# Prompt attention of a hybrid decoder step: queries split behind a shared transpose, and all eight key tiles of a group kept on chip

## The chip, the core and the metric

The kernel runs on one core of a Trainium2 chip, as one launch. The metric is device time in microseconds (us) of that core; the median of three runs stands for the kernel. A core has five engines with instruction queues of their own: TensorE (PE, with its weight loads shown as PEld), VectorE (DVE), ScalarE (ACT), GpSimd (POOL) and SyncE (SP), which here issues the DMA transfers. Each engine works through its queue in order and waits on semaphores.

## What is computed

One inference step of a two-layer decoder, for a prompt of 1024 rows and for 8 sample rows. Layer A is a gated delta rule with a convolution; layer B is sliding-window attention, and the change lies in layer B's part for the prompt. Cut to that:

```
def swa_layer(x, kb, vb, dist, valid, norm_g, w_in, q_norm, sinks, w_out):
    q, gate = jnp.split(rmsnorm(x, norm_g) @ w_in, 2, axis=-1)
    q = rmsnorm(q.reshape(b, L, N_Q_HEADS, HEAD_DIM), q_norm)          # 16 heads of 64
    q = q.reshape(b, n_blk, L // n_blk, N_KV_HEADS, Q_GROUP, HEAD_DIM) # 4 groups of 4 heads
    o = windowed_sink_attention(q, kb, vb, dist, valid, sinks).reshape(b, L, ATT_W)
    o = o * jax.nn.silu(gate)
    return x + o @ w_out

def windowed_sink_attention(q, k, v, dist, valid, sinks):
    s = einsum('bnqhgd,bnshd->bnhgqs', q, k) * HEAD_DIM ** -0.5
    s = where(valid, s - slopes * dist, -inf)          # a query block of 128 sees its own and the previous key block
    mx = maximum(max(s), sink); p = exp(s - mx)
    p = p / (sum(p) + exp(sink - mx))
    return einsum('bnhgqs,bnshd->bnqhgd', p, v)
```

Keys and values are projected once, from the residual stream behind layer A, for 4 key/value heads of 64; each is shared by a group of 4 query heads. All is float32.

## The kernel before, in words

**Precision.** A float32 product is made of passes over parts that the type float32r holds exactly: a value is copied to float32r (the high part, on ACT), the rest is subtracted (the low part, on DVE), and high times high, high times low and low times high are summed in PSUM. `split` (line 82) and `load_split` (line 87) do this for weights: the piece of 512 columns is loaded by SP, scaled by a gain on POOL (line 100), copied on ACT (line 83) and subtracted on DVE (line 84).

**The attention stage.** Behind layer A the program runs `load_qkv`, `sample_qkv`, `tile_qkv`, `gate_load` and `gate_group` over 4 groups of heads. Per group 256 columns of query weights, 64 of key and 64 of value weights are loaded and split (tile `wqkv`, two buffers), and the 1024 rows are taken in 8 tiles of 128. `tile_qkv` (line 1172) is a generator of three stages that the loop at line 1288 interleaves (`PIPE`): the stages of up to three tiles and the gate's projections (`gate_group`, 24 matmuls into the bank `ivY`) are issued alternately. The stages of tile t are:

1. 24 matmuls of 384 columns into `ps` (line 1178); the heads' mean squares (`head_stats`); the normed queries `qn`, 128 rows by 4 heads by 64 (DVE, line 1184); `qhl`, which puts each head's high part and low part side by side (high: ACT, line 1187; low: DVE, line 1188); the normed keys `kn`, twice side by side (DVE, line 1191). Then 4 transposes on PE, one per head, turn the 128 rows by (64 high + 64 low) into (64 high + 64 low) partitions by 128 rows, in PSUM (`tq`, line 1199), and ACT copies the 512 columns to `qst` (line 1201). The keys are transposed once (line 1203) and split into `kTh` (ACT, 1205) and `kTl` (DVE, 1206).
2. Scores: for each head two matmuls, `qst` against `kTh` and against `kTl` (lines 1225 and 1226). As `qst` holds high and low on two halves of the partitions and the keys stand on both halves, one matmul gives (high + low) times a part of the key. Then bias and maximum (DVE, 1229), exponentials and their scaling (ACT, 1239 and 1245).
3. Transposes of the probabilities in float32 (`ptp`, line 1252), copies (`pt`), and the product with the values (`op`, line 1262), which DVE multiplies into the gate (`oT`, line 1264).

**Keys on chip.** `kTh` and `kTl` hold `RK` = 4 tiles of 128 keys as a ring. A tile needs its own and the previous tile's keys. Where the two stand side by side the matmul has 256 columns; at t = 4 the ring wraps, the two are apart, and each head has four matmuls of 128 columns (`kcuts`, line 1208). At t = 0 there is no previous tile, and each head has two matmuls of 128.

**The output projection.** Tiles `oh` (line 1314) hold the attention's result of a row tile in parts; the weights `wob` come in three chunks of 384, 384 and 256 columns (line 1405). For each chunk and row tile: the residual is loaded (`hx5`, line 1419, two buffers; shown as `hx<-hD`), 24 matmuls run, DVE adds (line 1430) and SP stores (line 1435). The first tiles of the first chunk use the gate's one PSUM bank, the others two banks `pj`. PE starts on this while the last attention tiles are still in work.

**What sets the order.** In this stage the order of the instructions in each engine's queue is worked out when the program is built: a planner with costs of its own follows the program's order and lets an instruction ahead when the ones before it are still waiting. Buffers of closed pools are given to later pools, and a later tile waits for the last use of each earlier tile whose bytes it takes. On the left side of SBUF stand, in this order, the projected rows' inputs `ng` (24,576, 24,576 and 16,896 bytes a partition) with `hs` (1,280), then the attention's pool `at_`; behind them the output stage's 8 tiles `oh` take 65,536 bytes from the same start and the pool `p5` follows. `bp` (with `oT`, 32,768 bytes), the raw weights and the gate's weights `gw` (two buffers of 8,192) stand on the right side.

Of the kernel before, what the change touches and what calls it, by code (L numbers as in the profile page):

```python
# [20 lines left out]
P = 128  # L21
# [10 lines left out]
HD = 64  # L32
EPS = 1e-6
NEG = -1.0e30
RK = 4  # key tiles kept on chip
K1 = 6  # heads whose output is projected before the last two are done
# buffers
NB = 4  # half heads between their preparation and the chain
TFB = 2  # inverses ahead of the chain
QB = 3  # heads of convolved queries  # L40
NY = 3  # tiles of the last projection's first chunk that use the gate's bank
RB = [2, 2, 4]  # pieces of raw weights in flight: delta rule, output projection A, attention
LG = 2  # heads whose gate is projected last
# order of loads and of tiles
LO = "0g12k345q678"  # x's tiles, the norm's gain, the first key's and query's weights
CT = 5  # the x tile after which the convolution's taps are transposed
P3O = [0, 1, 2, 3, 8, 4, 5, 6, 7]
# stages of an attention tile and the tiles that each lags behind; the gate's tiles ahead
PIPE = [(1, 1), (0, 0), (2, 2)]
GA = 1  # L50
# what a stage's results are taken to need on the other engines (ns), and the priorities there
HOP = [1000, 900, 1200, 1000, 900, 1000, 900, 900]
# [6 lines left out]
def hybrid_step(  # L59
# [25 lines left out]

    # float32 products are three passes over parts that float32r holds exactly: hi * hi + hi * lo + lo * hi
    def load_split(hi, lo, src, gain=None):
        # src [P, k, c] in pieces of at most 512 a partition, scaled by gain [P, k] if there is one
        _, nk, c = src.shape
        n = min(512 // c, nk)  # L90
        for k in range(0, nk, n):
            pool = raws[-1]
            if len(raws) == 2:
                # both pools are open while the output projection's weights come in
                pool = raws[alt[0] % (RB[0] + RB[1]) >= RB[0]]
                alt[0] += 1
            raw = pool.tile([P, 512], F32, tag="raw", name="raw")[:, :n * c].rearrange("p (k c) -> p k c", c=c)
            DMA.dma_start(out=raw, in_=src[:, k:k + n])
            if gain is not None:
                G.tensor_tensor(out=raw, in0=raw, in1=gain[:, k:k + n].unsqueeze(2).broadcast_to([P, n, c]), op=ALU.mult)  # L100
            split(hi[:, k:k + n], lo[:, k:k + n], raw)
# [24 lines left out]

    # ---------------------------------------------------------------- constants
    ident = cst.tile([P, P], F32, name="ident")
# [4 lines left out]
    V.memset(ones, 1.0)  # L133
    # 1/sqrt(scale*src + eps): the first guess from the exponent's bits, a step of Newton's and one of third order
    NR0, NR1 = 2.38924456, 0.703952253
# [21 lines left out]

    # ---------------------------------------------------------------- phase 1: x -> normalised, transposed
    es2 = ExitStack()
# [9 lines left out]
    whl = es2w.enter_context(tc.tile_pool(name="whl", reuse_waits="tile", bufs=2, side="right"))  # L169
    # ---------------------------------------------------------------- phase 2a: decays, betas, taps  # L170
    p2 = es2.enter_context(tc.tile_pool(name="p2", reuse_waits="tile", bufs=1))
# [3 lines left out]
    mgtr = p2.tile([P, P], F32R, name="mgtr")  # L175
    # +1 on the diagonal, -1 right of it in the even rows: the inverse of the 2x2 blocks, transposed
    par = p2.tile([P, 1], F32, name="par")
# [231 lines left out]

    # ---------------------------------------------------------------- phase 2: projections, conv, delta rule  # L410
    gd = es2.enter_context(tc.tile_pool(name="gd", reuse_waits="tile", bufs=2))

    # The tensor engine's work from here to the output projection is cut into streams: generators that issue one stage
    # at a time and yield the time (ns) that the stage's results take on the other engines. run() merges them into the
    # tensor engine's order: a stage comes once its operands are due, and the projections fill the time between.
    due = {"decay": D0}
# [229 lines left out]
    def inverse(h):  # L646
# [3 lines left out]
        def clear(li):  # L650
            # zeroes what a level leaves unwritten in its blocks; the two tiles alternate
            b = lvls[li]
            z_ = xlv[li % 2].bitcast(F32)
            if b <= 16:
                z_ = z_.rearrange("p c (n s w) -> p c n s w", s=2, w=b // 2)[:, :, :, 1, :]
            G.memset(z_, 0.0)  # L656
# [154 lines left out]
    def norm_stream():  # L811
        for n_ in range(2 * H):
            h, hf = divmod(n_, 2)
            yield from need(("c", n_))
            d = dd[n_]
            osb, oss = d["osb"], d["oss"]
            # the query's norm enters only as the weight of the output norm's guard
            with tc.high_priority(offset=PN):
                x_ = sm.tile([P, 4], F32, tag="f1", name="f1")
                V.scalar_tensor_tensor(out=x_, in0=oss, scalar=NRS / 128.0, in1=d["xq"], op0=ALU.mult, op1=ALU.add)  # L820
                f2 = sm.tile([P, 4], F32, tag="f2", name="f2")
                u_ = sm.tile([P, 4], F32, tag="fu", name="fu")
                rsqrt_x(f2, x_, u_)
                V.tensor_tensor(out=osb, in0=osb, in1=f2.unsqueeze(2).broadcast_to(B4), op=ALU.mult)
            yield YN
            yield from need(("z", h))
            otp = gps("otp")
            for c in range(4):
                tr(otp[:, ts(c, P)], osb[:, c, :], ident)
            ov = hd[h]["og"][:, ts(hf, 512)]  # L830
            V.scalar_tensor_tensor(out=ov, in0=otp, scalar=ogain, in1=ov, op0=ALU.mult, op1=ALU.mult)
            yield (("n", n_), 700)
# [103 lines left out]

    # ---------------------------------------------------------------- phase 3: output projection A, residual, norm
    def zero_r(t_, scr):
# [126 lines left out]

    # ---------------------------------------------------------------- phase 4: shared K/V, q, gate, windowed attention
    bp = ctx.enter_context(tc.tile_pool(name="bp", reuse_waits="tile", bufs=1, side="right"))
# [29 lines left out]
    V.tensor_scalar_mul(distm, distm, -1.0)  # L1097
    identr = at_.tile([P, P], F32R, name="identr", bufs=1)
    V.tensor_copy(identr, ident)
    islp = at_.tile([P, NQH], F32, name="islp", bufs=1)  # L1100
# [16 lines left out]
    def gate_group(m, w_, gi):  # L1117
        # twice the gate's SiLU: g * (1 + tanh(g / 2)); the half goes into the product with the attention's output
        g0, gn = GRP[gi]
# [52 lines left out]
    def tile_qkv(g, t, w_):  # L1172
# [3 lines left out]
        for a, b in ((0, 0), (0, 1), (1, 0)):  # L1176
            for k in range(KT):
# [7 lines left out]
                        in1=r5[:, 0:4].unsqueeze(2).broadcast_to(s4), op=ALU.mult)  # L1185
        qhl = at_.tile([P, 4, 2, HD], F32R, tag="qhl", name="qhl", bufs=1)
        S.copy(qhl[:, :, 0, :], qn)
        V.tensor_tensor(out=qhl[:, :, 1, :], in0=qn, in1=qhl[:, :, 0, :].bitcast(F32), op=ALU.subtract)
        kn = at_.tile([P, 2, HD], F32, tag="kn", name="kn")
# [4 lines left out]
        if t == NT - 1:  # L1194
            DMA.dma_start(out=k_win_p[0, :, g, :], in_=kn[:, 0, :])
            DMA.dma_start(out=v_win_p[0, :, g, :], in_=vsb[:, t % 4, :])
        tq = chp.tile([P, 512], F32R, tag="chA", name="tq")
        for h in range(4):
            PE.transpose(tq[:, ts(h, P)], qhl[:, h].rearrange("p a d -> p (a d)"), identr)  # L1199
        qst = at_.tile([P, 512], F32R, tag="qst", name="qst")  # L1200
        S.copy(qst, tq)
        tk = ps[:, 384:512]
# [15 lines left out]
        for hp_ in range(2):  # L1218
            sps = gps("sps")
            s_ = at_.tile([P, 2, 2 * P], F32, tag="s_", name="s_", bufs=3)  # L1220
            for i in range(2):
                h = 2 * hp_ + i
                for k0, o_, nk in kcuts:
                    ov = sps[:, i * 256 + o_:i * 256 + o_ + nk]
                    mm(ov, qst[:, ts(h, P)], kTh[:, k0:k0 + nk], True, False)
                    mm(ov, qst[:, ts(h, P)], kTl[:, k0:k0 + nk], False, True)
            for i in range(2):
# [79 lines left out]

    # ---------------------------------------------------------------- sample attention and output projection B
    es5 = ExitStack()
# [95 lines left out]
    for ci, (c0, cn) in enumerate(CHK):  # L1405
# [10 lines left out]
        for t in list(range(NT)) + [NT]:  # L1416
            samp = t == NT
            n = NS if samp else P
            hx = bp.tile([P, 384], F32, tag="hx5", name="hx5", bufs=2)
            DMA.dma_start(out=hx[:n, :cn], in_=hD[t * P:t * P + n, c0:c0 + cn])  # L1420
# [48 lines left out]
```

## Time and profile before

| What | Value |
| --- | --- |
| Runs of the kernel (us) | 1325.66, 1326.26, 1332.1 |
| Median (us) | 1326.26 |
| Span of the profiled execution, first to last instruction (us) | 1323.5 |
| Mean granted TensorE clock in it, share of 2.4 GHz | 0.983 |
| Busy share of the span: PE, PEld, DVE, ACT, POOL | 93%, 85%, 72%, 48%, 23% |

The profiled execution is known by its span; the median of the runs is 2.8 us above it. Busy shares are means over stages with different limits. Matmuls are pipelined, and the duration that is shown for one runs to its modelled end, so what a matmul costs PE is read from the distance between starts. Where the profile says "idle before", the engine stood still, and the name behind the arrow is what ended the wait.

### The profile page before, as it was taken

The page shows a single profiled execution, that of the slowest core. Times are in us where ns is not written, and L with a number is a line of the kernel's source. Part 1 is how long each engine was busy: PE and PEld are TensorE (multiplying, and loading weights), DVE is VectorE, ACT ScalarE, POOL GpSimd, SP SyncE. Part 2 cuts the span into 40 slices and gives each one's busy share as a digit, 9 for nine tenths or more (in the row PEclk, how much of TensorE's full clock was granted, in tenths as well). Part 3 has the DMA queues.
Part 4 walks back from the last instruction along what each step waited for, and adds up shares of the span by engine and source line. Part 5 has one row for each costly group of instructions (what it writes and reads, how often), then busy time and mean ns, then how long its engine had stood idle before and what let it go on. Part 6 is the DMA issues. An engine that isn't in the chain of part 4 may idle for free.

```text
span 1323.5 us, 24515 instructions
## 1 busy us (share of the span) xinstructions
PE 1236.9 (93%) x8923; PEld 1122.8 (85%) x8923; DVE 949.1 (72%) x2897; ACT 635.6 (48%) x1822; POOL 299.1 (23%) x400
## 2 busy tenths in 40 slices
PE   4997989899999999998999999899999999999998
PEld 3987878898888899898887886798888888888898
DVE  7567878887888789888977548667686686777221
ACT  5343444635536455464654227365575575677100
POOL 1115442332334324344411002202011010000000
PEclk9998999999999999999999999999998999999999
DMA  7021201102021031110144437302011021102322
GB/s 249 19 65 32 58 25 50 51 17 84 17 84 33 17 85 30 56 49 17 51 143 144 149 134 244 87 26 56 4 50 32 3 57 31 45 1 72 128 90 72
DMA packets 124068, 87.89 MB, mean 66 GB/s; under 512 B 34152, under 2 KB 115792, under 8 KB 123888
## 3 DMA queue, kind: packets, MB, share of 16 engines
q1 hardware_dynamic: 123948, 86.33, 22.1%
q8 instruction: 70, 1.15, 0.4%
q14 instruction: 50, 0.41, 0.1%
HBM read 65.11 MB, written 23.28 MB: 67 GB/s over the span
## 4 chain that ended last, share of the span: by engine, by line
PE 63%; DVE 20%; ACT 8%; DMA 4%; issue 3%; POOL 2%; SPq 0%; ACTq 0%; DVEq 0%; POOLq 0%
PE pj L121 36%; DVE co L477 4%; PE ivt L121 3%; PE sps L121 3%; PE chB L121 2%; PE op L121 2%; PE chA L121 2%; PE ptp L1252 1%; DMA out_dram<-hx 1%; DVE wlo L84 1%; PE sp L121 1%; PE tq L1199 1%; ACT whi L83 1%; DVE wqkv L84 1%; ACT co L475 1%
## 5 line engine op out<-in xcount | busy, mean ns | idle before, releaser
L121 PE MATMUL pj<-xg,whi 128*128 128x384 f32 (+1 forms) x1536 | 311.7, 335 | 1.3 <-ACT whi L83 1.0
L121 PEld LDWEIGHTS pj<-xg,whi 128*128 128x128 f32 x1536 | 246.3, 192 | 2.6 <-ACT whi L83 1.2
L121 PE MATMUL pj<-xg,wlo 128*128 128x384 f32 (+1 forms) x768 | 164.7, 336 | 1.5 <-DVE wlo L84 1.5
L121 PE MATMUL pj<-wqkv,ng 128*128 128x384 f32 x768 | 155.6, 346 | 0.0
L477 DVE SCALAR_TENSOR_TENSOR co<-ue,cvT,co 128x528 f32<-128x528 f32 x144 | 128.6, 893 | 25.7 <-ACT co L475 24.3
L121 PEld LDWEIGHTS pj<-wqkv,ng 128*128 128x128 f32 x768 | 133.5, 190 | 5.0 <-issue 4.6
L121 PEld LDWEIGHTS pj<-xg,wlo 128*128 128x128 f32 x768 | 124.7, 192 | 2.8 <-DVE wlo L84 2.0
L121 PE MATMUL pj<-woa,ohl 128*128 128x512 f32 x384 | 105.7, 414 | 4.5 <-ACT ohl L83 2.2
L100 POOL TENSOR_TENSOR raw<-raw,gains 128x512 f32<-128x512 f32 x40 | 43.5, 1095 | 260.4 <-DMA raw<-in_w_in_b_dram 242.3
L121 PE MATMUL pj<-wob,oh 128*128 128x384 f32 (+1 forms) x576 | 99.6, 327 | 0.0
L121 PEld LDWEIGHTS pj<-wob,oh 128*128 128x128 f32 x576 | 92.1, 191 | 1.8 <-issue 1.5
L121 PEld LDWEIGHTS pj<-woa,ohl 128*128 128x128 f32 x384 | 69.3, 192 | 20.2 <-ACT ohl L83 2.7
L84 DVE TENSOR_TENSOR wlo<-raw,whi 128x512 fp32r<-128x512 f32 x64 | 56.1, 897 | 12.3 <-ACT whi L83 12.0
L1430 DVE TENSOR_TENSOR hx<-hx,pj 128x384 f32<-128x384 f32 (+3 forms) x27 | 13.7, 507 | 60.7 <-PE pj L121 37.0
L796 ACT ACTIVATE jk<-osb 128x128 bf16<-128x128 f32 x64 | 19.8, 309 | 71.9 <-DVE osb L791 64.2
L480 ACT ACTIVATE ue<-co 128x528 f32<-128x528 f32 x48 | 31.1, 647 | 44.0 <-DVE co L477 42.0
L482 POOL TENSOR_TENSOR ue<-ue,co 128x528 f32<-128x528 f32 x24 | 34.6, 1441 | 48.4 <-ACT ue L480 48.4
L226 ACT COPY ue<-pj 128x384 f32<-128x384 f32 x48 | 22.8, 475 | 42.4 <-PE pj L121 42.1
L656 POOL MEMSET xlv<- 128x256 f32 (+1 forms) x48 | 18.6, 389 | 103.7 <-PE ivt L121 85.4
L83 ACT CAST whi<-raw 128x512 fp32r<-128x512 f32 x64 | 38.1, 627 | 3.4 <-DMA raw<-in_w_in_a_dram 3.3
L121 PE MATMUL op<-pt,vsb 128*64 128x256 f32 x240 | 37.9, 396 | 1.0 <-DVE pt L1257 0.8
L785 DVE SCALAR_TENSOR_TENSOR st<-st,eG,chA 128x128 f32<-128x128 f32 x56 | 19.1, 342 | 26.6 <-PE chA L121 26.6
(904 smaller groups left out, 2920.9 us busy)
## 6 DMA issues: line engine op xcount, KB each, us to landing
raw<-in_w_in_a_dram SPq DMA_DIRECT2D x64, 256.0 KB
hD<-hx SPq DMA_DIRECT2D x16, 512.0 KB
raw<-in_w_in_b_dram SPq DMA_DIRECT2D x32, 256.0 KB
xt<-in_x_prompt_dram SPq DMA_DIRECT2D x8, 512.0 KB
ssm<-in_state_ssm_dram SPq DMA_DIRECT2D x8, 512.0 KB
out_dram<-ssm SPq DMA_DIRECT2D x8, 512.0 KB
raw<-in_w_out_a_dram SPq DMA_DIRECT2D x16, 256.0 KB
hx<-in_x_prompt_dram SPq DMA_DIRECT2D x8, 512.0 KB
```

What stands on the lines that cost most here:

```text
L83: S.copy(hi, raw)
L84: V.tensor_tensor(out=lo, in0=raw, in1=hi.bitcast(F32), op=ALU.subtract)
L100: G.tensor_tensor(out=raw, in0=raw, in1=gain[:, k:k + n].unsqueeze(2).broadcast_to([P, n, c]), op=ALU.mult)
L121: PE.matmul(out, lhsT, rhs, start=start, stop=stop, skip_group_check=True)
L226: S.copy(ue[:, 3 + g0:3 + g0 + gn], ps[:, :gn])
L477: V.scalar_tensor_tensor(out=cv, in0=ue[:, x * n + k:(x + 1) * n + k], scalar=cvT[:, m, 24 + k:25 + k], in1=cv, op0=ALU.mult, op1=ALU.add)
L480: S.activation(th, cv, AF.Tanh)
L482: G.tensor_tensor(out=th, in0=th, in1=cv, op=ALU.mult)
L656: G.memset(z_, 0.0)
L785: V.scalar_tensor_tensor(out=s_new, in0=s_old, scalar=eG[:, 2, h, cc:cc + 1], in1=psA[:, 128:256], op0=ALU.mult, op1=ALU.add)
L796: S.activation(jk, osb[:, c, :], AF.Square, accum_out=oss[:, c:c + 1])
L1430: V.tensor_tensor(out=hx[:n, :cn], in0=hx[:n, :cn], in1=ps[:n, :cn], op=ALU.add)
```

## The change

- The queries are no longer split ahead of the transposes. `qn` is transposed in float32, two heads at a time (64 + 64 columns), by two transposes instead of four, into a PSUM tile of 256 columns. Behind it the parts are made: for the even heads (partitions 0 to 63) ACT copies the high part to `qst`'s partitions 0 to 63 and DVE writes the low part to partitions 64 to 127; for the odd heads the halves are swapped. `qhl`, its copy and its subtraction, and the float32r identity `identr` go.
- `RK` is 8: the eight key tiles of a group stand side by side, and only t = 0 has matmuls of 128 columns.
- `hx5` moves from the pool `bp` (right side, open from the attention on) to `p5` (left side, opened behind it).

Apart from removed comments the diff is:

```diff
-RK = 4  # key tiles kept on chip
+RK = 8
...
-    identr = at_.tile([P, P], F32R, name="identr", bufs=1)
-    V.tensor_copy(identr, ident)
...
-        qhl = at_.tile([P, 4, 2, HD], F32R, tag="qhl", name="qhl", bufs=1)
-        S.copy(qhl[:, :, 0, :], qn)
-        V.tensor_tensor(out=qhl[:, :, 1, :], in0=qn, in1=qhl[:, :, 0, :].bitcast(F32), op=ALU.subtract)
...
-        tq = chp.tile([P, 512], F32R, tag="chA", name="tq")
-        for h in range(4):
-            PE.transpose(tq[:, ts(h, P)], qhl[:, h].rearrange("p a d -> p (a d)"), identr)
-        qst = at_.tile([P, 512], F32R, tag="qst", name="qst")
-        S.copy(qst, tq)
+        tq = chp.tile([P, 512], F32, tag="chA", name="tq")[:, :256].rearrange("p (j t) -> p j t", j=2)
+        for j in range(2):
+            PE.transpose(tq[:, j, :], qn[:, 2 * j:2 * j + 2].rearrange("p a d -> p (a d)"), ident)
+        qst = at_.tile([P, 4, P], F32R, tag="qst", name="qst")
+        qse = qst.rearrange("p (j e) t -> p e j t", e=2)
+        for e in range(2):
+            a_, b_ = slice(e * HD, e * HD + HD), slice(HD - e * HD, P - e * HD)
+            S.copy(qse[a_, e], tq[a_])
+            V.tensor_tensor(out=qse[b_, e], in0=tq[a_], in1=qse[a_, e].bitcast(F32), op=ALU.subtract)
...
-                    mm(ov, qst[:, ts(h, P)], kTh[:, k0:k0 + nk], True, False)
-                    mm(ov, qst[:, ts(h, P)], kTl[:, k0:k0 + nk], False, True)
+                    mm(ov, qst[:, h, :], kTh[:, k0:k0 + nk], True, False)
+                    mm(ov, qst[:, h, :], kTl[:, k0:k0 + nk], False, True)
...
-            hx = bp.tile([P, 384], F32, tag="hx5", name="hx5", bufs=2)
+            hx = p5.tile([P, 384], F32, tag="hx5", name="hx5", bufs=2)
```

## Rows read from the trace of the kernel before

**Rows 1.** Windows: attention stage, then a low-clock stretch; busy us (count), PEclk, DMA share, GB/s.

```profile
840.00:1226.00 386.00, 375.67 (x2398) 334.66 (x2396) 276.47 (x1103) 229.70 (x693) 35.63 (x34) 0.99 0.14 36
...
998.30:1005.10 6.80, 6.80 (x29) 6.70 (x29) 1.69 (x7) 0.65 (x2) 1.05 (x1) 0.50 0.17 39
```

**Rows 2.** The chain of waits from 840 us to the end, shares by line.

```profile
by line: PE pj L121 37.6%; PE sps L121 6.9%; PE op L121 5.9%; PE ptp L1252 3.7%; DMA out_dram<-hx 3.6%; PE tq L1199 2.2%; DVE wqkv L84 1.8%; DVE pt L1257 1.4%; DMA hx<-hD 1.3%; DVE ss L1145 1.2%; DVE qhl L1188 1.1%; DVE r L145 1.0%; issue 1
```

**Rows 3.** Timeline of PE around four transposes of queries: start us, us, what.

```profile
1147.85 2.56 PE L121 MATMUL pj<-wqkv,ng 128*128 128x384 f32 x13
1150.25 0.47 PE L1199 MATMUL tq<-identr,qhl 128*128 128x128 f32 x4
1150.55 0.59 PE L121 MATMUL pj<-wqkv,ng 128*128 128x384 f32 x2
1150.98 0.27 PE L1252 MATMUL ptp<-ident,s__14321 128*128 128x128 f32 x1
```

**Rows 4.** Timeline of PE: float32 transposes of probabilities, first and last of eight.

```profile
1192.85 0.38 PE L1252 MATMUL ptp<-ident,s__14826 128*128 128x128 f32 x2
...
1193.51 0.38 PE L1252 MATMUL ptp<-ident,s__14838 128*128 128x128 f32 x2
```

**Rows 5.** Timeline of PE, scores of t = 4: fifth of sixteen, and what follows them.

```profile
1094.02 0.28 PE L121 MATMUL sps<-kTh,qst 128*128 128x128 f32 x1
...
1095.36 1.45 PE L121 MATMUL pj<-wqkv,ng 128*128 128x384 f32 x7
```

**Rows 6.** The chain of waits, a stretch of scores with 256 columns.

```profile
1173.66 0.71 PE sps L121 x6
```

**Rows 7.** Waits of PE, 860 to 1226 us: total, times, longest.

```profile
PE tq L1199 <- DVE qhl L1188: 5.8, 6, 3.0
```

**Rows 8.** Timeline of all engines before the longest of these waits ends.

```profile
995.38 0.42 DVE L1184 TENSOR_TENSOR qn<-pj,r 128x256 f32<-128x256 f32 x1
...
995.72 0.47 DVE L1191 SCALAR_TENSOR_TENSOR kn<-pj,r,kgbc 128x64 f32<-128x64 f32 x2
995.84 0.41 ACT L1187 CAST qhl<-qn 128x256 fp32r<-128x256 f32 x1 [1.50 <-DVE qn L1184]
...
996.27 0.76 DVE L1188 TENSOR_TENSOR qhl<-qn,qhl 128x256 fp32r<-128x256 f32 x1
...
997.09 0.53 PE L1199 MATMUL tq<-identr,qhl 128*128 128x128 f32 x4 [3.00 <-DVE qhl L1188]
...
997.65 0.59 ACT L1201 CAST qst<-tq 128x512 fp32r<-128x512 f32 x1 [0.41 <-PE tq L1199]
```

**Rows 9.** Groups by line and shape: count | busy us, mean ns of one | idle before.

```profile
L1188 DVE TENSOR_TENSOR qhl<-qn,qhl 128x256 fp32r<-128x256 f32 x32 | 15.8, 493 | 4.1 <-ACT qhl L1187 3.7
L1184 DVE TENSOR_TENSOR qn<-pj,r 128x256 f32<-128x256 f32 x32 | 13.6, 424 | 1.0
L228 ACT COPY ue<-pj 128x256 f32<-128x256 f32 x24 | 8.9, 370 | 14.9 <-PE pj L121 14.8
L704 ACT CAST t<-ivt 32x256 f16<-32x256 f32 x16 | 5.8, 363 | 2.1 <-PE ivt L121 1.9
```

**Rows 10.** Timeline of DVE: four instructions that write to other partitions than they read.

```profile
1250.23 0.80 DVE L1398 TENSOR_TENSOR oTs<-po,oTs 64x32 f32<-64x32 f32 x4 [5.23 <-PE po L121]
```

**Rows 11.** Timelines of SP, PE and DVE: first loads of `hx5`, and towards the attention's end.

```profile
832.38 1.34 SPq L1420 DMA_DIRECT2D hx<-hD  x2
...
1139.70 65.97 SPq L1413 DMA_DIRECT2D raw<-in_w_out_b_dram  x5
...
1164.92 3.17 PE L121 MATMUL gps__14680<-ng,gw 128*128 128x264 f32 x24
...
1205.83 0.54 DVE L1430 TENSOR_TENSOR hx<-hx,pj 128x384 f32<-128x384 f32 x1
```

**Rows 12.** The chain of waits: a load of `hx5`.

```profile
1296.28 2.20 DMA hx<-hD
```

**Rows 13.** Groups of PE, 840 to 1226 us: the output projection's matmuls before the attention ends.

```profile
L121 PE MATMUL pj<-wob,oh 128*128 128x384 f32 x106 | 24.0, 357 | 0.0
```

## Prediction
> **What bounds the kernel now.** I read the windows first: in the attention stage, 840 to 1226 us, PE is busy 375.7 of 386 us, DVE 276.5 (72%) and ACT 229.7 (60%) [rows 1]. The reader is to see that only PE is full, so that an instruction taken off PE can come off the time, and one added on DVE mostly can not. The chain of waits says the same by lines: from 840 us on, `pj`, `sps`, `op` and `ptp`, all on PE, lead it, and of the lines that the change touches `sps` has 6.9%, `tq` 2.2% and `qhl` on DVE 1.1% [rows 2]. The last two are the interesting ones: they are there because PE stands behind them.
>
> Then I read what an instruction costs PE, from the distance between starts. Thirteen projections of 384 columns take 2.40 us up to the next start, 0.185 each. Four transposes of queries take 0.30 us from the first start to the next projection; the two projections behind them take 0.43 us where 0.37 would be usual, so the block costs 0.36 us [rows 3]. Float32 transposes start 0.11 us apart: six between 1192.85 and 1193.51 [rows 4]. Scores of 128 columns start 0.112 us apart (twelve between 1094.02 and 1095.36) [rows 5], those of 256 columns 0.118 us (six in 0.71) [rows 6]: half the columns save nothing.
>
> Last the waits. PE waited six times for the low part of the queries, 5.8 us in all, 3.0 at the longest [rows 7].
>
> **The change, part by part.**
>
> (a) *Two float32 transposes for four float32r ones.* Each of the 32 tiles gives up 0.36 us and takes 2 x 0.11 = 0.22: 0.14 to 0.15 us saved, times 32, **4.8 us**. If the new block leaves the same 0.06 us behind it that today's does, 0.08 us a tile or 2.6 us is left; that is the lower end, and I take the upper one, since the profile shows transposes of just this form and spacing. TensorE Precision Notes on the Trainium skill's page "FP8 and Floating Point Precision" speak against this step: a true float32 product is made of four passes through the array. By it the sum would come out as in the third rival below. The transposes shown here do not behave so.
>
> (b) *Eight key tiles.* At t = 4 of each of the 4 groups 16 matmuls of 128 columns become 8 of 256: 16 x 0.112 - 8 x 0.118 = 0.85 us, times 4, **3.4 us**. The t = 0 tiles keep theirs. No wait is added, as a ring of eight is written again a whole group later. I see no reason for another value; the ends are the same within a few tenths.
>
> (c) *The wait in front of the transposes.* At the longest wait `qn` ends at 995.80, ACT makes the high part from 995.84, DVE the low part from 996.27 to 997.03, PE starts at 997.09, and the copy to `qst` ends at 998.24 [rows 8]. Behind the change PE needs `qn` alone, 1.2 us earlier; the other five waits, 2.8 us together, are mostly shorter than that. The upper end is thus 1.2 + 2.8 = 4.0 us. What is late next is `qst`, for which the scores wait. Its chain from the end of `qn`: 0.56 us from the transposes' start to the copy's as today, two copies by ACT of 0.37, the second subtraction of 0.42, some 1.7 us with the hops, against 2.44 us today. So 0.7 us of the 1.2 stays where the scores come directly behind. I take **3.0 us**; the lower end is nothing.
>
> (d) *The clock.* Behind the 3.0 us wait the granted clock stood at 0.50 of 2.4 GHz, 1.2 GHz, for 6.8 us with PE busy throughout [rows 1]; that work would take 3.4 us less at the full clock. With a wait of about 1.8 us the fall may not come. Ends 0 and 3.4; I take the middle, **1.7 us**, as no row decides it.
>
> (e) *More on DVE, less on ACT.* An operation costs by its columns, not its partitions: 32 x 256 takes ACT 363 ns, 128 x 256 from PSUM 370 [rows 9]. So two copies of 64 x 256 (0.74 us) take the place of one of 128 x 256 and one of 128 x 512 (0.41 + 0.59) [rows 8]: ACT gains 0.26 us a tile, beside other work, worth nothing by itself. DVE had one subtraction of 493 ns in the mean; it gets two, for which `qn` with one input in PSUM, 424 ns, is the nearest row [rows 9]. The new ones write to other partitions than they read. Four instructions of that kind took 0.80 us, 0.20 each, one behind the other [rows 10], while ordinary ones overlap by 0.08 us (`qn` lasts 0.42, the next starts 0.34 after it) [rows 8]; with 0.08 for each of the two and for the one behind them a tile costs DVE 2 x 0.42 + 0.24 - 0.49 = 0.6 us more, 19 us in all. DVE is then busy some 295 of 386 us, 76%, and PE's own work covers it, save where DVE is full. That is so for about two tiles in each of the three groups in which the next group's weights are split during the tiles; the long wait above lies there. Six tiles times 0.6 would be 3.6 us, less what the old subtraction lost there (0.76 against 0.42) [rows 8]: I take **1.5 us lost**, ends 0 and 3.6. If PE's cover were gone throughout, the whole 19 us would show.
>
> (f) *`hx5` in `p5`.* Its first two loads are issued at 832.38 today and hold SP for 1.34 us [rows 11]. In `p5` they wait for earlier users of their bytes. From the shapes, `p5` starts 65,536 bytes behind the start of `ng`; its tiles ahead of `hx5` take 44,512; so `hx5` begins at 110,048, while the attention's pool ends at 67,328 + 30,272 = 97,600. It lies on the gate's second weight buffer, last read by the 24 matmuls from 1164.92, and it is first needed at 1205.83 [rows 11]. On SP the loads stand near five issues of raw weights that hold the queue from 1139.70 to 1205.67, waiting for a buffer [rows 11]: ahead of that wait they cost nothing, behind it the first lands 2.2 us later [rows 12], at 1207.9, 2.1 us after it is needed. I take **nothing**, since the gate's last matmuls end 35 us before the raw buffer comes free; the upper end is 2.1 us. Removing the two loads at 832 frees 1.3 us of SP, which waits for a raw buffer soon after, so nothing there either.
>
> The order in the queues is planned anew when the program is built. I price that at 0, with 3 us to either side.
>
> The sum: -4.8 - 3.4 - 3.0 - 1.7 + 1.5 = -11.4 us. It is made against a span of 1323.5 us, to 1312.1; the median of the runs lies 2.8 us above that span, which the change does not touch, so the prediction is 1326.3 - 11.4 = 1314.9, or **1315 us**.
>
> **The rivals.**
>
> *The wait moves to the scores.* The transposes start early, but the second copy and the second subtraction queue behind weight splits, and PE, which takes its queue in order, stands in front of `sps` instead. Then (c) and (d) give nothing and each of the six waits grows by 0.37 + 0.42 us: 8.2 - 4.7 = 3.5 us gained, 1322.8 us. For it: DVE is the engine that ended these waits. Against it: the new chain to `qst` is shorter by 0.7 us.
>
> *Slower: `hx5` blocks the end of the attention.* If its bytes lay on a tile of the attention still in use, the first DVE add could not run before 1226 us + 2.2 + 0.5. Today 106 matmuls of the output projection fill PE before 1226 [rows 13]; with the gate's one bank held, only the first 24 could run. 82 x 0.185 = 15.2 us and 2.7 us more would be lost, 17.9 - 11.4 = 6.5 us net, 1332.8 us. It decides as soon as that release comes after about 1206. Against it stands the count of bytes in (f).
>
> *Float32 transposes are dear.* If one cost as much as today's block of four, 0.36 us, two would cost 0.72 us: 0.36 more a tile, 11.5 us, and with the other terms unchanged +11.5 - 3.4 - 3.0 - 1.7 + 1.5 = +4.9, 1331 us. This is what the rule of the Trainium skill's page "FP8 and Floating Point Precision" named in (a) would make of it. The spacing of 0.11 us in [rows 4] speaks plainly against it.
>
> *The change does nothing measurable*, because PE is held by DVE and ACT all along the stage: 1326 us. PE's 97% busy speaks against it.
>
> **How the numbers follow.** The forecast 70%, the moved wait 20%, `hx5` 5%, dear transposes 2%, nothing 3%. The forecast's own range is 4.0 + 3.4 + 4.8 + 3.4 = 15.6 and 3 us of order below, 1307.7, to about 1319. The range takes in most of the moved wait: 1308 to 1325.5. About 0.5%, 6.6 us, is what a measurement here tells from no change. Faster by more than that holds the forecast and a little of the moved wait, 73%; within it the rest of that, the dear transposes and nothing, 22%; slower 5%.
>
> **What would show it.** Right: 64 float32 transposes of `qn` about 0.11 us apart; 32 score matmuls of 128 columns in place of 96; PE's waits for `qhl` gone and waits for `qn` under 3 us in all; no stretch at half clock near 1000 us; DVE some 290 to 300 us busy in the stage; the first `hx5` add around 1195 us. Wrong: waits of PE in front of `sps` that end on DVE or ACT and sum to 5 us or more; a PE gap behind 1190 us that ends on a load of `hx5`; distances of 0.2 us or more between the new transposes; a new stretch at half clock.

## The result and the profile after

The changed kernel is slower: 1338.99 us in the median of 4 runs (1338.74 to 1345.0), beside 1329.18 us for 4 runs of the kernel before on the same chip; the ratio is 1.0092 with a 95% interval of 1.0063 to 1.0121. 1315 us was predicted, and faster. The profiled execution took 1338.74 us, its span is 1336.7 us.

What was to be seen in the attention is there. The waits of PE from 860 to 1226 us, which answer to [rows 7] (total, times, longest):

```profile
PE ktps L1335 <- DMA kc__15199<-in_cache_k_win_dram: 8.9, 1, 8.9
...
PE sps L121 <- DVE qst L1201: 0.8, 2, 0.4
PE tq L1195 <- DVE qn L1182: 0.7, 3, 0.3
PE sps L121 <- ACT kTh L1205: 0.6, 2, 0.5
```

The 5.8 us in front of the transposes are 0.7, and no wait for the scores has taken their place. The first line is new and the largest: a wait behind the attention. The window leaves out one wait of 2.7 us for the first tile's `qn`, behind which 3.4 us run at 1.2 GHz; the kernel before waits 2.3 us for DVE in that place:

```profile
849.32 0.44 PE L1195 MATMUL tq<-ident,qn 128*128 128x128 f32 x2 [2.72 <-DVE qn L1182]
```

The new transposes, in the timeline of PE (start us, us, what), answer to [rows 3]:

```profile
1153.22 0.38 PE L1195 MATMUL tq<-ident,qn 128*128 128x128 f32 x2
1153.36 1.13 PE L121 MATMUL pj<-wqkv,ng 128*128 128x384 f32 x5
```

The first projection behind them starts 0.14 us after the first of the two. In the mean of the 32 tiles the next instruction of another kind starts 0.18 us behind the first transpose, where it was 0.33 us in the kernel before. The windows (as [rows 1]):

```profile
840.00:1226.00 386.00, 367.62 (x2254) 315.53 (x2253) 286.93 (x1150) 227.38 (x693) 36.39 (x34) 0.99 0.14 35
...
1219.10:1229.30 10.20, 3.97 (x18) 3.28 (x19) 1.26 (x6) 1.88 (x4) 0.47 (x1) 0.50 0.86 263
1243.00:1249.80 6.80, 6.15 (x20) 5.64 (x19) 1.22 (x5) 0.24 (x1) 0.00 (x0) 0.50 0.16 58
```

The low clock near 1000 us is gone, and two stretches at 1.2 GHz, of 10.2 and 6.8 us, stand at the end, where the kernel before has one of 3.4 us. DVE is busy 286.9 us in the stage, 10.5 more than before; of the groups of DVE the new subtraction has taken the place of the old one in [rows 9]:

```profile
L1201 DVE TENSOR_TENSOR qst<-tq,qst 64x256 fp32r<-64x256 f32 x64 | 27.0, 422 | 26.6 <-ACT qst L1200 25.1
```

The last product `op` of the attention comes at 1215.4 us, 9.5 us earlier than before (this line is of the kernel before):

```profile
1224.90 1.08 PE L121 MATMUL op<-pt,vsb 128*64 128x256 f32 x8
```

Most of that is work put off: 72 matmuls of the output projection stand ahead of it, where 105 did, and 33 at 0.185 us are 6 us. So some 3 us were won up to there, and more was lost behind it. Here are the groups of PE from 840 to 1226 us, `op` of the kernel before in the first line, the changed kernel in the other two (count | busy us, mean ns | idle before):

```profile
L121 PE MATMUL op<-pt,vsb 128*64 128x256 f32 x240 | 37.9, 396 | 1.0 <-DVE pt L1257 0.8
```

```profile
L121 PE MATMUL op<-pt,vsb 128*64 128x256 f32 x240 | 41.1, 395 | 2.3 <-DVE pt L1257 1.6 <-DVE e L1236 0.5
...
L121 PE MATMUL pj<-wob,oh 128*128 128x384 f32 x72 | 16.0, 353 | 0.0
```

Of the output projection 72 matmuls run before 1226 us, three tiles of 24, and not 106 [rows 13]; after that all banks were full, as no add had emptied one. The same 240 records of `op` keep PE 3.2 us longer: the second thing to explain. Now the end, on the timelines of SP's queue, PE and DVE:

```profile
1131.31 0.28 SPq L1164 DMA_DIRECT2D smqD<-qt  x1
1201.79 0.36 SPq L1190 DMA_DIRECT2D out_dram<-kn  x1
...
1204.62 13.89 SPq L1413 DMA_DIRECT2D raw<-in_w_out_b_dram  x21
...
1219.83 0.41 SPq L1328 DMA_DIRECT2D kc__15199<-in_cache_k_win_dram  x1
...
1222.15 1.36 SPq L1420 DMA_DIRECT2D hx<-hD  x2
```

```profile
1215.37 1.08 PE L121 MATMUL op<-pt,vsb 128*64 128x256 f32 x8 [0.68 <-DVE pt L1257]
1225.33 3.81 PE L1335 MATMUL ktps<-ident,kc__15199 128*128 128x128 f32 x16 [8.88 <-DMA kc__15199<-in_cache_k_win_dram]
```

```profile
1230.78 0.56 DVE L1430 TENSOR_TENSOR hx<-hx,pj 128x384 f32<-128x384 f32 x1 [10.28 <-DMA hx<-hD]
```

The first two loads of `hx5` went out at 832 us before [rows 11]; now they are the last of SP's queue there, behind the store of the last `kn` (it holds SP from 1131.6 to 1201.8 us), 21 raw weights (0.66 us each) and the loads of `smq` to `vc_`. The first add comes at 1230.8 in place of 1205.8 us. PE stands for 8.9 us, the clock falls, and it falls once more at 1243 us.

### The profile page after: what moved, and what is told of

It reads as the page before. It is cut to its first block, busy times and chain, and to the rows that moved or that the text cites. A ratio compares the mean times of both kernels' runs of the same rounds, so it can differ in the third digit from the quotient of the medians.

```text
span 1336.7 us, 24390 instructions
## 1 busy us (share of the span) xinstructions
PE 1236.6 (93%) x8827; PEld 1111.2 (83%) x8827; DVE 960.0 (72%) x2928; ACT 632.6 (47%) x1822; POOL 299.8 (22%) x400
## 4 chain that ended last, share of the span: by engine, by line
PE 60%; DVE 19%; ACT 8%; DMA 5%; issue 4%; POOL 3%; SPq 1%; DVEq 0%; POOLq 0%; ACTq 0%
PE pj L121 34%; DVE co L477 4%; PE ivt L121 3%; PE sps L121 2%; PE op L121 2%; PE chB L121 2%; PE chA L121 2%; DMA out_dram<-hx 1%; PE ptp L1252 1%; DVE wlo L84 1%; PE sp L121 1%; DMA hx<-hD 1%; ACT whi L83 1%; DVE wqkv L84 1%; ACT co L475 1%
## 5 line engine op out<-in xcount | busy, mean ns | idle before, releaser
L1201 DVE TENSOR_TENSOR qst<-tq,qst 64x256 fp32r<-64x256 f32 x64 | 27.0, 422 | 26.6 <-ACT qst L1200 25.1
L121 PE MATMUL op<-pt,vsb 128*64 128x256 f32 x240 | 41.1, 395 | 2.3 <-DVE pt L1257 1.6
```

Of the source, the lines that this page charges most:

```text
L121: PE.matmul(out, lhsT, rhs, start=start, stop=stop, skip_group_check=True)
L1201: V.tensor_tensor(out=qse[b_, e], in0=tq[a_], in1=qse[a_, e].bitcast(F32), op=ALU.subtract)
```

## The experiments

First theory (T): the place of `hx5`'s loads in SP's queue makes the loss. Rivals: A, the new queries or the eight tiles make it; B, it is the release of the bytes that `hx5` lies on. Ratios are to runs of the kernel before on the same chip, with their 95% interval. The runs come from several chips, on which that kernel's median is 1325.7 to 1329.2 us; a difference of two medians below has that uncertainty, and the difference of two ratios is the safer measure.

| Run | Median us | Ratio | Interval |
| --- | --- | --- | --- |
| e1 before, `hx5` moved | 1346.59 | 1.0137 | 1.0117 to 1.0157 |
| e2 changed, `hx5` in a pool of its own | 1324.85 | 0.9971 | 0.9954 to 0.9987 |
| e3 new queries alone | 1328.80 | 0.9997 | 0.9978 to 1.0015 |
| e4 changed, loads of `hx5` preferred | 1332.28 | 1.0029 | 1.0012 to 1.0045 |
| e5 e2 with six key tiles | 1329.59 | 1.0013 | 0.9994 to 1.0031 |
| e6 e2 with `op` kept together | 1311.95 | 0.9876 | 0.9844 to 0.9908 |
| e7 e6 with `kc_` on the gate's bytes | 1313.24 | 0.9886 | 0.9854 to 0.9918 |
| e8 before, `op` kept together | 1326.03 | 0.9988 | 0.9964 to 1.0011 |
| e9 changed, `op` kept together | 1335.65 | 1.0062 | 1.0039 to 1.0084 |
| e10 e3 with `op` kept together | 1321.34 | 0.9961 | 0.9945 to 0.9977 |
| e11 e6 with a third subtraction | 1319.77 | 0.9941 | 0.9919 to 0.9963 |
| e12 e6 with the scores kept together | 1310.71 | 0.9875 | 0.9851 to 0.9899 |
| e13 e6 with `op`'s partners apart | 1314.76 | 0.9922 | 0.9896 to 0.9948 |
| e14 e6 with six key tiles | 1321.76 | 0.9973 | 0.9953 to 0.9994 |
| e15 e6 with a copy of `kn` on POOL | 1312.75 | 0.9906 | 0.9882 to 0.9929 |

**Where the loads of `hx5` stand (e1, e2, e4).** The edit of e1, to the kernel before, and those of e2 and e4, to the changed kernel:

```diff
-            hx = bp.tile([P, 384], F32, tag="hx5", name="hx5", bufs=2)
+            hx = p5.tile([P, 384], F32, tag="hx5", name="hx5", bufs=2)
```

```diff
     es5 = ExitStack()
+    hxp = es5.enter_context(tc.tile_pool(name="hxp", reuse_waits="tile", bufs=1, side="right"))
...
-            hx = p5.tile([P, 384], F32, tag="hx5", name="hx5", bufs=2)
+            hx = hxp.tile([P, 384], F32, tag="hx5", name="hx5", bufs=2)
```

```diff
-            DMA.dma_start(out=hx[:n, :cn], in_=hD[t * P:t * P + n, c0:c0 + cn])
+            with tc.high_priority(offset=1000) if ci == 0 and t < 2 else ExitStack():
+                DMA.dma_start(out=hx[:n, :cn], in_=hD[t * P:t * P + n, c0:c0 + cn])
```

> The kernel before with hx5 in p5 and nothing else of the change. Theory (the loads of hx5 stand too late in SP's queue): the first two loads of hx5 are issued behind the load of vc_, after the end of the attention; the first add comes at 1228 to 1240 us, PE idles 8 us or more on kc_, and the kernel is 12 to 25 us slower than before, 1338 to 1351 us. Rival A (the loss comes from the new query preparation or the eight key tiles): within 3 us of before.

> The changed kernel with hx5 in a pool of its own, opened where the gate's pool closes; its bytes are still those of the gate's second weight buffer (184448 to 187520 in place of 181568 to 184640). Theory (place in the queue): the loads stand ahead of the last store of kn, the first add comes at 1193 to 1200 us, no wait of PE on kc_ above 3 us, and the time is 1311 to 1321 us. Rival B (it is the release of the gate's bytes that comes late): first add at 1220 us or later and no gain, 1335 to 1342 us. Rival A: 1333 us or more.

> The changed kernel, hx5 in p5 at the same bytes, but its first two loads are given priority: they stand behind the raw weights and directly ahead of the loads of smq to vc_, not behind them. Theory: the first load is issued some 4 us earlier than in the changed kernel (about 1218.5 in place of 1222.2), the first add comes 4 to 8 us earlier, and the time lies between the changed kernel and the one with a pool of its own, 1325 to 1336 us. Rival B: the same as the changed kernel, 1337 to 1341 us.

The one line of e1 costs 18.2 us (1.37% by the ratio), with no other part of the change. The first add comes at 1237.1 us, as T has it; PE waits 5.7 us for `kc_`, less than the 8 that T asked for. Its loads on SP's timeline, its wait of PE and its low clock:

```profile
1228.95 1.58 SPq L1420 DMA_DIRECT2D hx<-hD  x2
```

```profile
PE ktps L1335 <- DMA kc__15297<-in_cache_k_win_dram: 5.7, 1, 5.7
```

```profile
1225.00:1242.10 17.10, 10.35 (x50) 8.38 (x51) 3.57 (x26) 4.13 (x9) 0.00 (x0) 0.50 0.53 171
```

That the change as a whole lost only 9.8 us (0.92% by the ratio) means that its other parts gained, as e1 alone loses more. In e2 `hx5` lies on bytes of the same gate buffer as in the changed kernel, so B would have it slow; SP's timeline shows the loads 59 us earlier:

```profile
1163.47 0.82 SPq L1421 DMA_DIRECT2D hx<-hD  x2
1203.36 0.34 SPq L1190 DMA_DIRECT2D out_dram<-kn  x1
```

The first add is at 1205.3 us (1193 to 1200 was expected), the wait for `kc_` is 1.9 us, and the kernel is 14.1 us faster than the changed one. B falls, and T stands. The run e4 is in between, as T has it: bytes as in the changed kernel, loads at 1220.94 us, directly ahead of `smq` instead of behind `vc_`, first add at 1223.99 us, 6.7 us faster than the changed kernel. But e2 missed the 1311 to 1321 us that T gave: 1324.85. Something else took away some 10 us of what was forecast.

**What the queries alone bring (e3) and the tiles alone (e5).** e3 is the changed kernel with `RK = 4` and `hx5` in `bp`; e5 is e2 with `RK = 6`, where t = 6 has the 16 short scores that t = 4 had before.

> The change's queries alone: four key tiles on chip and hx5 where it was. By the prediction's terms, -4.8 for the transposes, -3.0 and -1.7 for the wait and the clock, +1.5 for DVE: 8 us less than before, 1318 us, 1312 to 1323. Rival A (the second subtraction on DVE costs): 1326 us or more.

> The kernel of e2 (hx5 in a pool of its own) with six key tiles on chip in place of eight, so that each group has a second tile whose 16 scores have 128 columns: term (b) alone. By that term 3.4 us slower than e2, whose median was 1324.9: 1328 us (1326 to 1330). Rival (PE is held by waits, and shorter scores give nothing): 1324 to 1326 us.

e3 gives nothing (0.03%, 0.19 either way) although PE waits for `qn` just twice, 0.4 us in all, from 860 to 1226 us. e5 is 4.7 us slower than e2 by medians, 0.42% with 0.25 either way by the ratios: (b) is there. So the missing time had to be in what e2 and e3 share. Comparing starts on PE showed it: the product with the values, `op`, is cut up more often. A tile has four products, each shown as two records. In the timeline of e2 (the lone ones are "x2"), then of the kernel before:

```profile
1070.41 1.40 PE L121 MATMUL pj<-wqkv,ng 128*128 128x384 f32 x7
1071.73 0.65 PE L121 MATMUL op<-pt,vsb 128*64 128x256 f32 x2
1072.56 0.44 PE L1195 MATMUL tq<-ident,qn 128*128 128x128 f32 x2 [0.18 <-DVE qn L1182]
1072.92 0.65 PE L121 MATMUL op<-pt,vsb 128*64 128x256 f32 x2
1073.50 0.79 PE L121 MATMUL pj<-wqkv,ng 128*128 128x384 f32 x3
```

```profile
1073.33 0.65 PE L121 MATMUL op<-pt,vsb 128*64 128x256 f32 x4
1073.92 1.00 PE L121 MATMUL gps__13504<-ng,gw 128*128 128x264 f32 x6
```

One product holds PE for 0.58 us (1072.92 to 1073.50), two for 0.59, and four for 1.01. The kernel before has 5 lone products; the changed kernel, e2 and e3 have 17. The blocks sum to 34.8 us before and 38.3 in e2. In e2's lines the planner has put the next tile's transposes between two products.

**Keeping `op` together (e6, e8), and `kc_` early (e7).** Theory D: the missing gain went into the new order. Rival E: DVE's longer chain holds PE. The edit, in e6 to e2 and in e8 to the kernel before; e7 has `kc_` in `hxp` too:

```diff
+        with tc.high_priority(offset=1000):
-        for kt in ks_:
+            for kt in ks_:
...
```

> The kernel of e2 with a higher priority for the four products op of a tile. In the order that the planner made for e2 17 of these products stand alone on PE and in the kernel before 5; one alone takes 0.58 us, and two that write the two halves of op take 0.58 us together. With the priority none stands alone (8 pairs and 26 fours). Theory D (the missing gain of e2 went into the new order): 17 x 0.58 + 8 x 0.58 + 5 x 1.01 + 18 x 1.01 = 37.7 us become 8 x 0.58 + 26 x 1.01 = 30.9 us, so 4 to 7 us faster than e2: 1318 to 1321 us. Rival E (DVE's longer chain holds PE, and the time moves into other waits): within 2 us of e2, 1323 to 1327 us.

> The kernel before with the same priority for op and nothing else. There 5 products stand alone; by theory D 34.8 us of op become 24 x 0.58 + 18 x 1.01 = 32.1 us, 2.7 us faster at most: 1323 to 1328 us. Rival (the priority itself helps, whatever the number of lone products): 5 us or more, 1323 us or less.

> As e6, and the tile kc_ in the pool of hx5, on the gate's bytes, so that its load needs not wait for the attention's end. Theory: PE's wait of 1.9 us for kc_ in e2 goes, 1 to 4 us faster than e6: 1315 to 1319 us. Rival (the end has other work to wait for): the same as e6.

e6 is 12.9 us faster than e2, where D gave 4 to 7, and 16.3 us faster than the kernel before by medians (1.24% by the ratio), the best of this study with e7 and e12. The groups of PE in e6, to 1240 and to 1226 us:

```profile
L121 PE MATMUL op<-pt,vsb 128*64 128x256 f32 x240 | 33.5, 393 | 1.0 <-DVE e L1236 0.7 <-DVE pt L1257 0.2
```

```profile
L121 PE MATMUL pj<-wob,oh 128*128 128x384 f32 x174 | 36.6, 348 | 0.2 <-DVE hx L1432 0.2
```

No product stands alone, the blocks sum to 31.2 us, 7.1 less than in e2, and 174 matmuls of the output projection are done by 1226 us, where e2 had done 131. From the first transposes of queries to PE's last matmul e6's profile is 10.0 us shorter than e2's; what `op` does not explain of that is spread over small waits, 1.2 us of it in front of `kc_`. The same priority gives the kernel before 0.12%, with 0.23 either way: it had little to mend. With the new queries it gives 7.5 us at four key tiles (e10 against e3) and 7.8 at six (e14 against e5), by medians. So the priority is no general gain; it takes back what the new order had cost. E's claim that the time would move to other waits fails. e7 changes nothing against e6: the wait for `kc_` is 0.7 us there already.

**Both faults apart (e9), the queries again (e10).** e9 is the changed kernel and e10 is e3, each with the priority.

> The changed kernel with the priority for op and hx5 still in p5. Theory: two causes that add. In the order of the queues the loads of hx5 stand behind vc_ still, so 10 us or more of the loss at the end stays; the lone products of op go. 5 to 13 us faster than the changed kernel (1339.0), 1326 to 1334 us, and 14 to 22 us slower than e6. Rival (the late loads hide whatever the attention gains): 1337 to 1341 us.

> The kernel of e3 (the new queries alone, four key tiles, hx5 where it was) with the priority for op. Against e8, which is the kernel before with the same priority (1326.0 us). By the terms (a), (c), (d) and (e) of the prediction 8 us less: 1318 us, 1314 to 1322. Rival E (DVE's longer chain takes the gain back, whatever the order): 1324 us or more.

e9 gained 3.3 us, less than expected and more than the rival allowed; by the ratios it is 0.30% with 0.37 either way, so that it gained anything is not shown. Its windows and waits at the end suggest why the two costs don't add:

```profile
1195.00:1250.00 55.00, 42.81 (x210) 36.84 (x209) 19.16 (x81) 17.56 (x49) 3.36 (x4) 0.72 0.28 87
```

```profile
PE ktps L1336 <- DMA kc__15199<-in_cache_k_win_dram: 5.6, 1, 5.6
PE ptp L1252 <- ACT s__14966 L1245: 3.6, 1, 3.6
```

PE reaches the full banks earlier, and waits and the low clock (0.72 in the mean over 55 us) take most of what the attention gained; that is read from one profile. e10 is 4.7 us faster than e8 by medians, where 8 was forecast; by the ratios it is 3.6, with 3.8 either way.

**DVE's chain (e11, e15) and the scores (e12).** The edits to e6: in e11 the second subtraction is written twice; in e15 POOL copies `kn`'s second half in place of DVE; in e12 the scores begin with the operands that come last:

```diff
             V.tensor_tensor(out=qse[b_, e], in0=tq[a_], in1=qse[a_, e].bitcast(F32), op=ALU.subtract)
+            if e:
+                V.tensor_tensor(out=qse[b_, e], in0=tq[a_], in1=qse[a_, e].bitcast(F32), op=ALU.subtract)
```

```diff
...
+        G.tensor_copy(kn[:, 1, :], kn[:, 0, :])
```

```diff
-            for i in range(2):
+            for i in (1, 0):
...
+                    mm(ov, qst[:, h, :], kTl[:, k0:k0 + nk], True, False)
+                    mm(ov, qst[:, h, :], kTh[:, k0:k0 + nk], False, True)
```

> The kernel of e6 with one more subtraction of 64 x 256 a tile on DVE, which writes the same rows again: 32 x 0.42 = 13.5 us more busy time of DVE in front of the scores. By term (e), 1.5 us lost for 19 us, about 1 us slower than e6: 1312 to 1315 us. Rival E (DVE's chain is on the path of the scores): 5 us slower or more, 1317 us or more. If DVE's time counted in full: 1325 us.

> The kernel of e6 in which a tile's scores begin with the operands that come last (kTl and the second head of a pair), so that the order holds them in 37 blocks in place of 68. In e6 33 blocks of two took 0.32 us each, 12 of four 0.51, 21 of six 0.80 and 2 of eight 1.21: 36.0 us; eight together take 1.03 in the kernel before. Theory D (broken blocks cost PE): 2 to 4 us faster than e6, 1307.5 to 1310.5 us. Rival (PE then stands in front of the block for the last operand, 32 times): the same or slower, 1311.5 to 1317 us.

> The kernel of e6 in which the second copy of kn is made by POOL from the first, so that DVE gives up 32 x 0.27 = 8.7 us of busy time a tile's chain. Theory (DVE's chain costs 0.6 us for each us, as in e11): up to 5 us faster than e6, 1306 to 1310 us. Rival (POOL's copy is late for the transposes of kn, and the order breaks the blocks more often): slower than e6, 1313 to 1320 us.

e11 took 7.8 us more than e6 (0.65%, 0.39 either way) for this much DVE time, and PE's waits for the scores (860 to 1226 us) grew from 0.9 us:

```profile
L1203 DVE TENSOR_TENSOR qst<-tq,qst 64x256 fp32r<-64x256 f32 x32 | 13.6, 426 | 1.0
```

```profile
PE sps L121 <- DVE qst L1203: 2.1, 5, 0.6
```

That is about 0.6 us for each us of DVE; the waits that the profile names are only a part, and blocks of scores and transposes are cut more often as well, so the rate holds the order's share too. E is right in this: DVE in front of the scores is not hidden. e12 gave nothing. The blocks of scores got fewer and take 33.1 us for 35.4, and the waits moved to the transposes, 3.3 us in e6:

```profile
PE tq L1195 <- DVE qn L1182: 6.7, 6, 2.6
```

So for the scores D's gain is taken back by waits; it shows in the time for `op` alone. e15 stayed at e6's time too (0.30% slower, 0.40 either way). DVE's busy time in the stage fell from 287.4 to 282.2 us, less than the 8.7 reckoned, and that brought nothing; so e11's rate does not hold for every part of DVE's chain.

**Why a lone product is dear (e13), and the tiles again (e14).** The products of a tile write two halves of `op`, partitions 0 to 63 and 64 to 127. e13 turns their loops, so that neighbours in the queue write the same half; e14 is e6 with `RK = 6`.

```diff
-            for kt in ks_:
-                for a in range(2):
+            for a in range(2):
+                for kt in ks_:
```

> The kernel of e6 with the four products of a tile in another order: both products of the first half of op, then both of the second, so that neighbours write the same half. Theory (two products that write different halves run side by side): a block of four takes 2.0 us in place of 1.02, 28 such tiles and 4 with two products: some 28 to 32 us more on PE, 1336 to 1345 us. Rival (a lone product is dear for another reason, the switch of forms): within 3 us of e6, 1309 to 1315 us.

> The kernel of e6 with six key tiles on chip in place of eight. By term (b) 3.4 us slower than e6: 1314 to 1317 us. If eight tiles are worth the 9.4 us between e10 and e6: 1320 us or more.

e13 is 2.8 us slower than e6 by medians (0.46% by the ratios, 0.41 either way), not 28. In 16 of its 26 blocks of four, products that stand together still take 1.02 to 1.05 us, as on its timeline here:

```profile
1137.93 1.09 PE L121 MATMUL op<-pt,vsb 128*64 128x256 f32 x8
1138.95 1.67 PE L121 MATMUL pj<-wqkv,ng 128*128 128x384 f32 x8
```

That does not refute the theory of partners side by side, whose price of 28 us took for granted that the new order keeps the halves apart. The starts of the records show that it does not. The two records of a lone product start 0.27 us apart; in this block a second record starts 0.007 us behind the first, as in e6, so it is another product's (the timeline cut at 1137.945 us):

```profile
1137.93 0.44 PE L121 MATMUL op<-pt,vsb 128*64 128x256 f32 x2
```

Of the other blocks five take 1.15 to 1.22 us. In the last five the queue's second product, which writes the first one's half, came late, as its operand was not yet there. PE runs the first alone and starts the next two within 0.08 us of each other, and the block takes three steps in place of two, 1.42 to 1.58 us:

```profile
1076.61 1.51 PE L121 MATMUL op<-pt,vsb 128*64 128x256 f32 x8
1078.05 0.62 PE L121 MATMUL gps__13598<-ng,gw 128*128 128x384 f32 x2
```

So products of the two halves run side by side, in either order of the queue, once their operands are there. A lone product takes as long as a pair, and three (1.01 us) as long as four, as one half has no work meanwhile. e13's blocks sum to 35.1 us, 3.9 more than e6's, which is the size of its loss. Beside this there is a price for each entry and exit: from the last record of `op` to the next instruction of another kind it takes 0.31 us in nearly every block of every run, where the later records of one half start 0.22 us apart. The Trainium skill's page "TensorEngine Tiling (Array Packing)" says under Key Properties that a change of tiling mode drains TensorE, and `op`, with 64 columns of weights, stands among products with 128. The rows of the exit agree with that; no run here separates the drain from other causes.

e14 is 9.8 us slower than e6, nearer to the 9.4 us between e10 and e6 than to the 3.4 of term (b).

## Why the prediction was wrong, step by step

- **(f), the step that failed first.** It said that the loads would cost nothing, "since the gate's last matmuls end 35 us before the raw buffer comes free" (38 by [rows 11]). The bytes were right: the gate's buffer was free by 1163.5 us, as e2's loads into it show. But the step priced the release and only two places in SP's queue, ahead of or behind the raw loads. The planner put them at a third, behind the store of `kn`, 21 raw loads and all loads of `p5`. Moving `hx5` alone costs 18.2 us (e1), mending its place alone gives 14.1 us (e2). The slower rival had the right end, adds after 1226 us, banks full, PE without work, and asked for the wrong condition: bytes on the attention's tiles. It also let 24 matmuls run, where 72 did.
- **"The order in the queues is planned anew", priced at 0 with 3 us to either side: failed.** Lone products of `op` went from 5 to 17. Mending that gives 12.9 us with the change (e6 against e2) and 2.2 us without it (e8), so the new order cost some 10 us with eight tiles; the pairs with four and six tiles (7.5 and 7.8 us) make it some 5. That the priority does nothing else is not shown: the blocks of `op` explain 7.1 of the 12.9 us.
- **(a) right, near its upper end.** From the first transpose to the next other instruction 0.33 us became 0.18: 4.8 us in 32 tiles, as forecast. Counted with the longer distance that follows, where the rows allow it, 0.40 became 0.28, an estimate of 3.8 us; the new block too leaves something behind it. The rule of four passes (the Trainium skill, "FP8 and Floating Point Precision", TensorE Precision Notes) does not show in these transposes: two of them start 0.11 us apart where they follow each other, and 128 columns take 0.06 us at the projections' 0.185 us for 384: about twice that, not four times.
- **(b) right in sign; the size is open.** Between starts, waits over 0.3 us left out, all scores take 37.9 us in e5 and 35.3 in e2: 2.6 us of work for the 3.4 forecast. In the runs e5 against e2 gives 0.42% (0.25 either way), e14 against e6 0.97% (0.38 either way, or 8 to 18 us), more than the matmuls alone. The planner's order differs in each pair, and no run separates it.
- **(c) right.** 5.8 us of waits became 0.7 in the same window; with the first tile's 2.7 us the waits for `qn` are 3.4 us from 840 us on, a little over the prediction's mark of 3. The rival in which the wait moves to the scores did not come: its mark was 5 us, and the profile has 1.6 us of waits of `sps`.
- **(d) consistent, its cause open.** The 6.8 us at half clock near 1000 us are in [rows 1] and again in e1 (996.3 us), both with the old queries and their order; no profile with the new queries has them. The length of the wait alone does not decide it: in e1 one of 2.1 us goes with a stretch at 1.2 GHz, and in e8, with the old queries, one of 2.5 us at the same place goes with none; in the changed kernel the 2.7 us in front of the first `qn` go with 3.4 us, in e2 2.6 us there with none. What the term left out came behind the attention: 10.2 and 6.8 us at 1.2 GHz.
- **(e) mis-sized.** DVE's two subtractions take 27.0 us where one took 15.8 [rows 9]: 11.2 us more, which is the forecast's 2 x 0.42 - 0.49 a tile. The rest of its 19 us is lost overlap, which no busy time holds; the trace has it, as DVE's next instruction starts 0.03 us behind the end of a new subtraction and 0.08 us ahead of the end of `qn`. What failed is the share that shows: at e11's rate the 11.2 us are worth 7 us, 3 to 11 with its interval (an estimate), where 1.5 was taken and 3.6 was the upper end. The step let only the six tiles with weight splits count; that the chain to the scores is tight in the others too is likely and not shown.

With `hx5`'s place and `op`'s order mended, e6 is 14.1 us faster than e8, which has the same priority; the forecast for (a) to (e) was 11.4. That the two come close is partly luck: the queries gave 4.7 us for 8 (e10 against e8), and the eight tiles, with `hx5` in its own pool, 9.4 for 3.4 (e6 against e10). The change was worth making; what it moved along with it was not priced.

## What to carry to other kernels

A load that moves to another pool has two dates, when its bytes are free and when its turn in the queue comes; price the second by everything that the queue issues between, stores that wait included. Where a planner orders the work, a piece that is ready earlier cuts up what it overtakes, so count how often short products stand alone before and after; a priority that keeps them together can be worth more than the change. Before you call an engine hidden, ask whether its work is in front of the bottleneck's next operand, not only how busy it is.

## What was not expected of the hardware

- A lone product of 128 x 256 with 64 weight columns holds PE for 0.58 us, two that write different halves for 0.58 and four for 1.01 (e2, e6): the two start 0.007 us apart and run side by side, in e13 too, where the neighbours in the queue write the same half.
- A wait of PE of 8.9 us cost more than itself: a stretch at 1.2 GHz that began within it lasted 10.2 us, and 17.1 us in e1, with PE busy for 4.0 and 10.4 us of them. In the prediction the clock stood only among the gains.
- In the changed kernel SP issues nothing between 1131.6 and 1201.8 us, while 21 raw loads and 2 of `hx5`, among others, are queued behind one store. The Trainium skill's page "DMA: Bandwidth & Descriptors" says, in its section on the anatomy of one DMA, that DMA engines do not wait on semaphores and that the issuing engine does so before it dispatches. The trace agrees.
